# A two-layer decoder trunk on one core: DMA transposes for the second chunk of FFN parts too, and an out product ordered by chunks

## The chip, the cores and the metric

The kernel runs on one core of a Trainium2 chip. The metric is the device time of one execution in microseconds; the time before is a median of three runs. A core has TensorE (PE, matmuls and transposes), VectorE (DVE), ScalarE (ACT), GpSimd (POOL), and SyncE (SP), which here only issues DMAs.

## The reference

```python
for i in range(DEPTH):                      # 2 layers, x is 512 x 1024 float32
    h = h + 0.5 * swiglu(rms_norm(h, ffn1_norm[i]), ffn1_w_in[i], ffn1_w_out[i])
    hn = rms_norm(h, mix_norm[i])
    m = recurrent_mixer(...) if i % 2 == 0 else spatial_gating_mixer(...)
    h = h + m
    h = h + 0.5 * swiglu(rms_norm(h, ffn2_norm[i]), ffn2_w_in[i], ffn2_w_out[i])
return rms_norm(h, final_norm)

def swiglu(x, w_in, w_out):                 # w_in 1024 x 5632, w_out 2816 x 1024
    g, u = jnp.split(x @ w_in, 2, axis=-1)
    return (jax.nn.silu(g) * u) @ w_out
```

There are four FFN calls (two in each layer), and the change touches only them.

## The kernel before

**Products.** Every large matrix product is done as seven products of half-size blocks (a Strassen form, `seven`, L376): P1 P2 P5 P6 P3 P7 Q4, whose left sides are the blocks A11, A12, A22 of the left matrix and the sums S1 = A21 - A22, S2 = S1 - A11, S3 = -S2 - A22, S4 = S2 + A12 (L47, L48). The right sides are blocks of weights and their sums, made by an accumulating DMA on POOL (L139) or by an add on VectorE (L166). Each float32 operand is split into a high part (`hi`, `whi`, a copy on ScalarE) and the rest (`lo`, `wlo`, a subtract on VectorE, L103, L104, L185, L186), and each block product is three matmuls: high by high, low by high, high by low (L423 to L425). A product collects in PSUM banks A, B or C, and P6, P3 and P7 go on adding in the banks that P1 and P5 have filled (L49), once VectorE or ScalarE has read these.

**An FFN call** is cut into three parts (`FF_PARTS`, L31). Part 1 has a narrow pair and a chunk of four blocks of 128 columns; parts 2 and 3 have two chunks of four. A chunk (`chunk`, L804) runs the seven products of x with two halves of 512 rows (two entries of `cuts`), 14 steps of 12 matmuls each. Its end is the gated activation, rows of tokens, in four tiles (128 tokens by 512 columns): the first two after P3 (`p3`, L830), the other two after Q4 (`q4`, L841). After both chunks comes the part's out product (`out_blocks`, L640), again 14 steps, P1 of the first chunk, P1 of the second, P2 of the first and so on: its left side is the activation with the columns on the partitions, so the tiles have to be transposed.

**Two ways to transpose** (`left_blocks`, L752). The first chunk of parts 2 and 3, and the pair, go by the DMA (`cross`, L298): ScalarE takes the float32 tile apart into two planes of 16 bits (`planes`, L302), SyncE issues a transposing DMA for each (`move`, L310), ScalarE puts the planes together again (`merge`, L318), and VectorE makes S1 from A21 and A22 (`s1`, L322). The second chunk goes over TensorE (`stage`, L335, `turn`, L262): 16 transposes of 128x128 in two runs of eight, one step after P3 and one after Q4; ScalarE copies the result out of PSUM, and VectorE makes S1 on the way (`take`, L271). Either way `parts` (L348) then splits the block into hi and lo.

**Order.** All is issued in an order that is written by hand. The list `subs` holds the steps; the main loop (L1629) goes through them. In step i it first runs the functions hooked to "pre", then splits the weights of step i + 3, then runs "mid" and "rest", issues weight loads (L136) while fewer than eight raw buffers are in use, issues the matmuls of step i, then runs "end", the step's own work after its matmuls (`post`) and "late". Every engine works through its instructions in this order. There are four buffers of split weights, so whi of step i + 3 can be written when step i - 1 is done. `out_blocks` hooks the splits of S2, S4, S3 and A22 two steps ahead of the products that use them (three or four in some places, L732 to L736), and `sums` (L789) hooks the making of S2, S4 and S3.

**After the out product** of the last part, a norm follows (`BlockNorm.quarter`, L544): when P2 is through, ScalarE squares a quarter of x, TensorE transposes it, and so on for the other quarters.

Of the kernel before, what the change touches and what calls it, by code (L numbers as in the profile page):

```python
# [10 lines left out]
U16 = mybir.dt.uint16  # L11
# [42 lines left out]
def trunk(ctx: ExitStack, tc: tile.TileContext, a: dict, out: bass.AP):  # L54
# [13 lines left out]
    def nm(s):  # L68
        uid[0] += 1
        return f"{s}_{uid[0]}"  # L70
# [25 lines left out]
    def act(o, x, f, **k):  # L96
        nc.scalar.activation(out=o, in_=x, func=f, **k)  # L97
# [151 lines left out]
    class Group:  # L249


        def __init__(self, n):
            self.n, self.f, self.hl = n, {}, {}

        def new(self, name):
            self.f[name] = slot(name=name.lower())[:, : self.n * H]
# [38 lines left out]
            for c, g in cs:  # L295
                stt(lo[:, c], ps[:, c], g, f32(hi[:, c]), ALU.mult, ALU.subtract)

        def cross(self, n, names, tiles):  # L298

            w, pl, dt = 4 * self.n * P, [], {}  # L300

            def planes():  # L302
                for h in tiles:
                    t = sp.tile([P, 2 * T], U16, tag="s", name=nm("pl"))[:, :w]
                    act(t.rearrange("p (k b f) -> p k b f", k=2, b=2),
                        h.bitcast(U16).rearrange("p (k f b) -> p k b f", k=2, b=2), AF.Copy)
                    pl.append(t)
                tiles.clear()

            def move():  # L310
                for name, k in names:
                    d = dt[name] = sp.tile([P, 2 * T], U16, tag="s", name=nm("dt"))[:, :w]
                    v = d.rearrange("p (m s t) -> p m s t", s=2, t=P)
                    for s, t in enumerate(pl):
                        nc.sync.dma_start_transpose(out=v[:, :, s, :], in_=t[:, k * w // 2 : (k + 1) * w // 2])
# [9 lines left out]
            hook(n, "mid", planes)  # L325
            hook(n, "rest", move)
            for i, (name, _) in enumerate(names):
                hook(n + 3 + i, "mid", lambda name=name: merge(name))
                if name in ("A11", "A12"):
                    hook(n + 5 + i, "mid", lambda name=name: self.parts(name))  # L330
            if names[-1][0] == "A21":
                hook(n + 5, "pre", s1)
                hook(n + 5, "mid", lambda: self.parts("S1"))

        def stage(self, n, name, src, gains=None, parts=True, where=None, direct=0, turn=None, lag=0):  # L335

# [579 lines left out]
    def ffn(w_in, w_out, norm):  # L916
        f0 = 0
        for i, sizes in enumerate(FF_PARTS):
            groups, p0, pair, first = [], f0, None, not subs
            for j, n in enumerate(sizes):  # L920
# [10 lines left out]
            last, mixed = i == len(FF_PARTS) - 1, "p" in sizes  # L931
# [3 lines left out]
            gs = out_blocks(w_out, p0, [g.n for g in groups], 0.5, norm if last else None, own=True, soon=soon,  # L935
                            swap=mixed, p2_lag=6 * mixed)
            gs.update(enumerate(groups))


# [732 lines left out]
```

## Time and profile before

| what | value |
|---|---|
| median of three runs | 1595.22 us (1595.11 to 1600.31) |
| the profiled execution's own time | 1601.47 us |
| its span, first to last instruction | 1599.8 us |
| granted TensorE clock | 0.999 |
| DMA transposes issued by SyncE | 96 |
| share of 16 DMA engines: SyncE's queue, POOL's queue | 40.0%, 34.4% |

A group row reads: line, engine, operation, out<-in, shapes, count | busy us, mean ns of one | idle time of the engine just before, and what ended it. A row of a timeline reads: start us, length us, engine, line, operation, names, shapes, count, and in brackets the idle time before it. A row of waits reads: who waited for whom: us in total, times, the longest. Matmuls overlap, so the listed length of one is more than the time from one to the next. L97 and L88 are the helpers through which ScalarE and VectorE operations go.

### The profile page before, as it was taken

Reading aid. Unit: us, or ns where it says so; the run is one execution under the profiler, and the core shown is the slowest. Engines: PE = TensorE matmul, PEld = TensorE weight load, DVE = VectorE, ACT = ScalarE, POOL = GpSimd, SP = SyncE. Lnnn points to the kernel's source line nnn. Section 1 sums busy time; section 2 is a strip of 40 time slices with the busy share of each in tenths; the row PEclk is TensorE's granted clock in tenths of the full one; section 3 lists DMA queues with packets and bytes.
Section 4 is the critical chain, followed back from the end, with each engine's and each line's share of the span. In section 5 each row is a group of like instructions: output and inputs, shape, how many; then the busy total and the mean of one; then the engine's idle time right before and its main releaser. Section 6 shows DMA issues by size and latency. Waiting matters only on the chain.

```text
span 1599.8 us, 20767 instructions
## 1 busy us (share of the span) xinstructions
PE 1585.2 (99%) x7293; PEld 1314.5 (82%) x7293; DVE 1368.5 (86%) x1834; ACT 1098.4 (69%) x1567; POOL 223.1 (14%) x201
## 2 busy tenths in 40 slices
PE   9999999999999999999999999999999999999998
PEld 7778888898888888888788888888888888888886
DVE  6898897888998897877888978878978988889788
ACT  7757657668777657557677576576886875675676
POOL 2111111100010111111102111111211011111120
PEclk9999999999999999999999999999999999999999
DMA  8779978853294788978838788778878657796793
GB/s 287 175 170 185 226 168 193 213 150 103 82 215 104 175 189 196 220 173 174 213 112 185 177 192 213 178 179 215 226 196 207 158 127 196 179 221 173 173 223 104
DMA packets 208297, 289.79 MB, mean 181 GB/s; under 512 B 55505, under 2 KB 81217, under 8 KB 208193
## 3 DMA queue, kind: packets, MB, share of 16 engines
q1 hardware_dynamic: 158688, 195.33, 40.0%
q0 software_dynamic: 47712, 91.30, 34.4%
q10 hardware_dynamic: 1792, 1.84, 0.4%
q8 instruction: 57, 0.93, 0.2%
q14 instruction: 48, 0.39, 0.1%
HBM read 275.84 MB, written 2.10 MB: 174 GB/s over the span
## 4 chain that ended last, share of the span: by engine, by line
PE 90%; DMA 4%; DVE 3%; issue 1%; ACT 1%; SPq 0%; POOL 0%; ACTq 0%; DVEq 0%; POOLq 0%
PE A L425 13%; PE A L424 13%; PE A L423 13%; PE C L424 7%; PE C L425 7%; PE C L423 7%; PE p L870 4%; PE B L425 4%; PE B L424 4%; PE B L423 4%; PE e L268 2%; PE r L226 2%; PE r L228 2%; PE r L227 2%; DMA raw<-in_ffn_w_in_dram 2%; DMA dt<-pl 1%
## 5 line engine op out<-in xcount | busy, mean ns | idle before, releaser
L88 DVE TENSOR_TENSOR wlo<-raw,whi 128x1024 fp32r<-128x1024 f32 (+1 forms) x537 | 639.2, 1194 | 170.9 <-ACT whi L97 164.6
L97 ACT ACTIVATE whi<-raw 128x1024 fp32r<-128x1024 f32 (+1 forms) x537 | 553.7, 1034 | 324.6 <-PE A L424 81.1
L423 PE MATMUL A<-whi,hi 128*128 128x512 f32 x1016 | 399.0, 393 | 0.8 <-ACT c L97 0.8
L425 PE MATMUL A<-wlo,hi 128*128 128x512 f32 x1016 | 396.0, 390 | 0.0
L424 PE MATMUL A<-whi,lo 128*128 128x512 f32 x1016 | 395.8, 390 | 0.0
L425 PEld LDWEIGHTS A<-wlo,hi 128*128 128x128 f32 x1016 | 190.7, 188 | 40.1 <-DVE wlo L88 0.4
L423 PEld LDWEIGHTS A<-whi,hi 128*128 128x128 f32 x1016 | 190.9, 188 | 39.6 <-ACT c L97 1.2
L424 PEld LDWEIGHTS A<-whi,lo 128*128 128x128 f32 x1016 | 190.9, 188 | 38.8 <-DVE lo L88 0.3
L424 PE MATMUL C<-whi,lo 128*128 128x512 f32 x560 | 218.8, 391 | 1.2 <-DVE lo L88 1.2
L423 PE MATMUL C<-whi,hi 128*128 128x512 f32 x560 | 219.1, 391 | 0.7 <-ACT hi L97 0.7
L425 PE MATMUL C<-wlo,hi 128*128 128x512 f32 x560 | 218.7, 390 | 0.0
L139 POOL DMA_DIRECT2D raw<-in_ffn_w_in_dram x82 | 99.1, 1216 | 718.2 <-DMA raw<-in_ffn_w_out_dram 302.6
L139 POOL DMA_DIRECT2D raw<-in_ffn_w_out_dram x72 | 83.3, 1196 | 376.5 <-DVE wlo L88 152.4
L88 DVE TENSOR_TENSOR raw<-raw,raw 128x1024 f32<-128x1024 f32 x108 | 129.8, 1202 | 0.5
L88 DVE TENSOR_TENSOR lo<-a,hi 128x512 fp32r<-128x512 f32 (+1 forms) x188 | 123.0, 662 | 2.9 <-ACT hi L97 2.8
L424 PEld LDWEIGHTS C<-whi,lo 128*128 128x128 f32 x560 | 105.5, 188 | 23.9 <-DVE lo L88 2.0
L97 ACT ACTIVATE hi<-a 128x512 fp32r<-128x512 f32 (+1 forms) x188 | 111.9, 600 | 18.8 <-DVE a L88 16.6
L423 PEld LDWEIGHTS C<-whi,hi 128*128 128x128 f32 x560 | 105.4, 188 | 23.1 <-ACT hi L97 1.1
L425 PEld LDWEIGHTS C<-wlo,hi 128*128 128x128 f32 x560 | 105.6, 188 | 21.9
L424 PE MATMUL B<-whi,lo 128*128 128x512 f32 x280 | 109.1, 390 | 0.1
L423 PE MATMUL B<-whi,hi 128*128 128x512 f32 x280 | 109.1, 390 | 0.0
L425 PE MATMUL B<-wlo,hi 128*128 128x512 f32 x280 | 109.0, 389 | 0.0
(183 smaller groups left out, 2102.7 us busy)
## 6 DMA issues: line engine op xcount, KB each, us to landing
raw<-in_ffn_w_in_dram SPq DMA_DIRECT2D x161, 512.0 KB, 4.5
raw<-in_ffn_w_out_dram SPq DMA_DIRECT2D x100, 512.0 KB, 5.0
raw<-in_ffn_w_in_dram POOLq DMA_DIRECT2D x82, 512.0 KB, 6.7
raw<-in_ffn_w_out_dram POOLq DMA_DIRECT2D x60, 512.0 KB, 7.8
raw<-in_sg_w_in_dram SPq DMA_DIRECT2D x20, 512.0 KB, 6.7
raw<-in_ffn_w_in_dram SPq DMA_DIRECT2D x34, 256.0 KB, 5.1
raw<-in_rec_w_in_dram SPq DMA_DIRECT2D x16, 512.0 KB, 3.9
raw<-in_sg_w_in_dram POOLq DMA_DIRECT2D x12, 512.0 KB, 8.4
```

Of the source, the lines that this page charges most:

```text
L88: nc.vector.tensor_tensor(out=o, in0=x, in1=y, op=op)
L97: nc.scalar.activation(out=o, in_=x, func=f, **k)
L139: nc.gpsimd.dma_start(out=self.v, in_=src, accum_op=ALU.add)
L226: nc.tensor.matmul(ps, wh, xh, start=start, stop=False)
L227: nc.tensor.matmul(ps, wh, xl, start=False, stop=False)
L228: nc.tensor.matmul(ps, wl, xh, start=False, stop=stop)
L268: nc.tensor.transpose(ps[:, o : o + P], src(q, s), ident)
L423: nc.tensor.matmul(ps, zh, wh, start=fresh and i == 0, stop=False, **k)
L424: nc.tensor.matmul(ps, zl, wh, start=False, stop=False, **k)
L425: nc.tensor.matmul(ps, zh, wl, start=False, stop=end, **k)
L870: nc.tensor.matmul(bank_of(half, s), z, (sub.lo if m == 2 else sub.hi)[:, q, :], start=left[2] == "2" and (h, q, m) == (0, 0, 0), stop=lef ...
```

## The change

Three things change. (1) The second chunk of parts 2 and 3 (`late`, not in the last part of the last call) uses the DMA transposes too, with its own times: for the first half the planes come one step after P3, its merges in steps 0 and 1 of the out product, its splits in steps 1 and 2; for the second half the planes come right behind the gate, the merges at the ends of steps 3 and 5, the split of S1 in step 4. (2) The out product of these parts takes the steps in the order `APART`, so that the second chunk's P1 is step 3 (was 1), P2 step 4 (was 3), P5 step 6 (was 5), while the first chunk's P5 and P6 come at 2 and 5 (were 4 and 6). (3) In `cross` itself, for all chunks that use it: plane copies are of half a tile each, and each transpose is issued behind its own copy; S1 is made by VectorE before the planes, from the two column halves of a tile (two subtracts of 128x256); merges write in one run and read the two planes in turn (they read in one run and wrote every second 16 bits before); and for the first chunks merges, splits and sums come two steps later.

```diff
+APART = [("P1", 0), ("P2", 0), ("P5", 0), ("P1", 1), ("P2", 1), ("P6", 0), ("P5", 1), ("P6", 1), ("P3", 0), ("P3", 1),
+         ("P7", 0), ("P7", 1), ("Q4", 0), ("Q4", 1)]
...
-        def cross(self, n, names, tiles):
-            w, pl, dt = 4 * self.n * P, [], {}
-            def planes():
-                for h in tiles:
-                    t = sp.tile([P, 2 * T], U16, tag="s", name=nm("pl"))[:, :w]
-                    act(t.rearrange("p (k b f) -> p k b f", k=2, b=2),
-                        h.bitcast(U16).rearrange("p (k f b) -> p k b f", k=2, b=2), AF.Copy)
-                    pl.append(t)
+        def cross(self, half, tiles, planes, merges, parts):
+            w, names = 2 * self.n * P, ("A12", "A11") if half == 0 else ("S1", "A22")
+            if half == 0:
+                names = names[::-1]
+            dt = {}
+            def move():
+                pl = [sp.tile([P, 2 * T], U16, tag="s", name=nm("pl"))[:, : 2 * w] for _ in tiles]
+                for k, name in enumerate(names):
+                    c = slice(k * w, (k + 1) * w)
+                    d = dt[name] = sp.tile([P, 2 * T], U16, tag="s", name=nm("dt"))[:, : 2 * w]
+                    v = d.rearrange("p (m s t) -> p m s t", s=2, t=P)
+                    for s, (t, h) in enumerate(zip(pl, tiles)):
+                        act(t[:, c].rearrange("p (b f) -> p b f", b=2),
+                            h.bitcast(U16)[:, c].rearrange("p (f b) -> p b f", b=2), AF.Copy)
+                        nc.sync.dma_start_transpose(out=v[:, :, s, :], in_=t[:, c])
                 tiles.clear()
-            def move():
-                for name, k in names:
-                    d = dt[name] = sp.tile([P, 2 * T], U16, tag="s", name=nm("dt"))[:, :w]
-                    v = d.rearrange("p (m s t) -> p m s t", s=2, t=P)
-                    for s, t in enumerate(pl):
-                        nc.sync.dma_start_transpose(out=v[:, :, s, :], in_=t[:, k * w // 2 : (k + 1) * w // 2])
-                pl.clear()
             def merge(name):
-                t = self.new("S1" if name == "A21" else name)
-                act(t.bitcast(U16).rearrange("p (x b) -> p b x", b=2), dt.pop(name).rearrange("p (b x) -> p b x", b=2), AF.Copy)
-            def s1():
-                tt(self.f["S1"], self.f["S1"], self.f["A22"], ALU.subtract)
+                act(self.new(name).bitcast(U16).rearrange("p (x b) -> p x b", b=2),
+                    dt.pop(name).rearrange("p (b x) -> p x b", b=2), AF.Copy)
...
         n = now[0] + lag
+        if g.late:
+            e = now[0] + (0 if half else 4)
+            hs = [tiles[2 * half + s] for s in range(2)]
+            if half:
+                for h in hs:
+                    tt(h[:, : g.n * P], h[:, : g.n * P], h[:, g.n * P :], ALU.subtract)
+                g.cross(half, hs, (e, "late"), ((e + 4, "rest"), (e + 6, "rest")), [(e + 5, "mid")])
+                sums(g, e + 6)
+            else:
+                g.cross(half, hs, (e - 3, "mid"), ((e + 1, "mid"), (e + 2, "mid")), ((e + 2, "mid"), (e + 3, "mid")))
+            return
         if whole:
-            g.cross(n, (("A22", 1), ("A21", 0)) if half else (("A11", 0), ("A12", 1)),
-                    [tiles.pop(2 * half + s) for s in range(2)])
+            hs = [tiles[2 * half + s] for s in range(2)]
             if half:
-                sums(g, n + 6)
+                for h in hs:
+                    tt(h[:, : g.n * P], h[:, : g.n * P], h[:, g.n * P :], ALU.subtract)
+                sums(g, n + 8)
+            g.cross(half, hs, (n, "mid"), ((n + 5, "mid"), (n + 6, "mid")), [(n + 7, "mid"), (n + 8, "mid")][: 2 - half])
             return
...
+                    groups[-1].late = j == 1 and not mixed and not (last and hasattr(norm, "last"))
...
+            gs = out_blocks(w_out, p0, [g.n for g in groups], 0.5, norm if last else None,
+                            APART if groups[1].late else None, own=True, soon=soon, swap=mixed, p2_lag=6 * mixed)
```

More of the change, by code (lines that the diff above doesn't have):

```diff
@@ L252, in __init__ @@
         def __init__(self, n):
-            self.n, self.f, self.hl = n, {}, {}
+            self.n, self.f, self.hl, self.late = n, {}, {}, False
         def new(self, name):
@@ L296, in direct @@
                 stt(lo[:, c], ps[:, c], g, f32(hi[:, c]), ALU.mult, ALU.subtract)
-        def cross(self, n, names, tiles):
-            w, pl, dt = 4 * self.n * P, [], {}
-            def planes():
-                for h in tiles:
-                    t = sp.tile([P, 2 * T], U16, tag="s", name=nm("pl"))[:, :w]
-                    act(t.rearrange("p (k b f) -> p k b f", k=2, b=2),
-                        h.bitcast(U16).rearrange("p (k f b) -> p k b f", k=2, b=2), AF.Copy)
-                    pl.append(t)
-                tiles.clear()
-            def move():
-                for name, k in names:
-                    d = dt[name] = sp.tile([P, 2 * T], U16, tag="s", name=nm("dt"))[:, :w]
-                    v = d.rearrange("p (m s t) -> p m s t", s=2, t=P)
-                    for s, t in enumerate(pl):
-                        nc.sync.dma_start_transpose(out=v[:, :, s, :], in_=t[:, k * w // 2 : (k + 1) * w // 2])
-                pl.clear()
-            def merge(name):
-                t = self.new("S1" if name == "A21" else name)
-                act(t.bitcast(U16).rearrange("p (x b) -> p b x", b=2), dt.pop(name).rearrange("p (b x) -> p b x", b=2), AF.Copy)
-            def s1():
-                tt(self.f["S1"], self.f["S1"], self.f["A22"], ALU.subtract)
[L325 to L333, printed above, removed]
@@ new lines, in cross @@
+        def cross(self, half, tiles, planes, merges, parts):
[13 more added lines that the diff above has]
+                        nc.sync.dma_start_transpose(out=v[:, :, s, :], in_=t[:, c])
+                tiles.clear()
+            def merge(name):
+                act(self.new(name).bitcast(U16).rearrange("p (x b) -> p x b", b=2),
+                    dt.pop(name).rearrange("p (b x) -> p x b", b=2), AF.Copy)
+            hook(*planes, move)
+            for name, at in zip(names, merges):
+                hook(*at, lambda name=name: merge(name))
+            for name, at in zip(names, parts):
+                hook(*at, lambda name=name: self.parts(name))
@@ L919, in ffn @@
             groups, p0, pair, first = [], f0, None, not subs
+            last, mixed = i == len(FF_PARTS) - 1, "p" in sizes
             for j, n in enumerate(sizes):
@@ L934, in ffn @@
             soon = {("Q4", 1): 3} if last and isinstance(norm, TileNorm) else {}
-            gs = out_blocks(w_out, p0, [g.n for g in groups], 0.5, norm if last else None, own=True, soon=soon,
-                            swap=mixed, p2_lag=6 * mixed)
+            gs = out_blocks(w_out, p0, [g.n for g in groups], 0.5, norm if last else None,
+                            APART if groups[1].late else None, own=True, soon=soon, swap=mixed, p2_lag=6 * mixed)
             gs.update(enumerate(groups))
```

1 line of the change is left out of this document (removed).

## The prediction

> **What bounds the kernel now.** I read the page's engine busy times first, then its chain.
>
> ```profile
> span 1599.8 us, 20767 instructions
> PE 1585.2 (99%) x7293; PEld 1314.5 (82%) x7293; DVE 1368.5 (86%) x1834; ACT 1098.4 (69%) x1567; POOL 223.1 (14%) x201
> PE 90%; DMA 4%; DVE 3%; issue 1%; ACT 1%; SPq 0%; POOL 0%; ACTq 0%; DVEq 0%; POOLq 0%
> ```
>
> TensorE is busy 99% of the span and carries 90% of the chain: what leaves its queue is gained, and what makes it wait is lost. VectorE is close behind. Next, the waits of TensorE, all the transposes of FFN blocks, and a stretch of the chain in order of time:
>
> ```profile
> PE e L268 <- DVE c L94: 4.0, 8, 1.1
> ```
>
> ```profile
> L268 PE MATMUL e<-ident,c 128*128 128x128 f32 x224 | 30.7, 274 | 4.0 <-DVE c L94 4.0
> ```
>
> ```profile
> 656.52 0.87 PE e L268 x8
> ```
>
> Eight of these transposes take 0.87 us on the chain, 0.109 each (the 274 ns of the group are overlapped lengths). The only sizeable waits of TensorE stand before them. Then the busy time of each engine in one out product, that of part 2 of the second FFN call (its second chunk ends at 653.64):
>
> ```profile
> 653.64:689.89 36.25, 36.25 (x165) 30.11 (x164) 34.54 (x45) 19.69 (x25) 4.82 (x4) 1.00 0.81 204
> ```
>
> The columns are PE, PEld, DVE, ACT, POOL busy, then clock, DMA share, GB/s. TensorE has no gap, but VectorE is busy 34.54 of 36.25 us: this is the stage where the change puts its work, and VectorE has hardly anything left there.
>
> **What is removed.** Seven second chunks become "late" (parts 2 and 3 of the four FFN calls, less the very last). Each loses 16 transposes on TensorE: 7 x 2 x 0.87 = **12.2 us**. Of the waits, those of late chunks are
>
> ```profile
> 292.84 0.55 PE L268 MATMUL e<-ident,c 128*128 128x128 f32 x3 [0.50 <-DVE c L94]
> ```
>
> ```profile
> 644.64 0.98 PE L268 MATMUL e<-ident,c 128*128 128x128 f32 x7 [0.55 <-DVE c L94]
> ```
>
> ```profile
> 761.07 0.30 PE L268 MATMUL e<-ident,c 128*128 128x128 f32 x1 [0.25 <-DVE c L94]
> 762.37 0.99 PE L268 MATMUL e<-ident,c 128*128 128x128 f32 x7 [1.00 <-DVE c L94]
> ```
>
> 0.50 + 0.55 + 0.25 + 1.00 = **2.3 us**. If nothing else were late, the gain would be 14.5 us.
>
> **What is added, and its prices.**
>
> ```profile
> L97 ACT ACTIVATE whi<-raw 128x1024 fp32r<-128x1024 f32 x507 | 535.0, 1058 | 318.9 <-PE A L424 79.0 <-DVE raw L88 72.1 <-PE C L424 68.6
> L88 DVE TENSOR_TENSOR wlo<-raw,whi 128x1024 fp32r<-128x1024 f32 x507 | 618.5, 1223 | 164.7 <-ACT whi L97 158.4 <-PE e L268 4.1 <-PE A L425 1.4
> L97 ACT ACTIVATE hi<-a 128x512 fp32r<-128x512 f32 x168 | 103.8, 623 | 18.8 <-DVE a L88 16.6 <-DVE a L94 1.0
> L88 DVE TENSOR_TENSOR lo<-a,hi 128x512 fp32r<-128x512 f32 x168 | 114.6, 690 | 2.9 <-ACT hi L97 2.8
> L88 DVE TENSOR_TENSOR raw<-raw,raw 128x1024 f32<-128x1024 f32 x104 | 127.0, 1221 | 0.5
> L94 DVE SCALAR_TENSOR_TENSOR x<-A,x 128x512 f32<-128x512 f32 x112 | 71.8, 689 | 6.4 <-PE A L425 6.3
> L88 DVE TENSOR_TENSOR a<-y,h 128x256 f32<-128x256 f32 x16 | 5.8, 422 | 0.0
> L97 ACT ACTIVATE pl<-h 128x512 uint16<-128x512 uint16 x16 | 9.0, 612 | 0.0
> L97 ACT ACTIVATE pl<-c 128x1024 uint16<-128x1024 uint16 x32 | 32.9, 1054 | 2.7 <-DVE c L94 2.6
> L97 ACT ACTIVATE a<-dt 128x1024 uint16<-128x1024 uint16 x24 | 32.9, 1372 | 19.0 <-DMA dt<-pl 18.8
> L97 ACT ACTIVATE junk<-x 128x512 f32<-128x512 f32 x55 | 34.1, 625 | 7.8 <-DVE x L94 7.5
> L97 ACT ACTIVATION_READ_ACCUMULATOR junk<-x 128x1 f32 x55 | 10.5, 191 | 0.0
> ```
>
> Per late chunk ScalarE gets 8 plane copies of 128x512 (0.61 us) and 4 merges, and loses three copies from PSUM; VectorE gets two 128x256 subtracts (0.42) for one 128x512 operation. The merge in its new order (one run written, two planes read in turn) isn't in the trace. Its bounds are 1.05 (plane copy: strided read, one written run) and 1.37 (old merge: strided write); I take 1.05, since what the change turns round is the write, as in the plane copy. The Trainium skill ("Advanced Engine Details and Errata", SBUF Cachelines) says that an access which leaves the 16-byte line each time pays a penalty; the new merge's read does. No row here shows that case; it is a rival below.
>
> The first chunks change too: two plane copies become four of half size (2.1 to 2.4 us), merges and parts two products later. Their merges now wait 19.0 us for the DMA on ScalarE; that wait goes, but TensorE never waited there but for the transposes counted above, so I cost it at nothing. The cover is the weight splits made three products ahead, 8 us; were that gone, TensorE would see at most those 19 us, and they get fewer, not more.
>
> SyncE's queue: 56 more DMA transposes stand ahead of later loads.
>
> ```profile
> SPq L136 <- DVE wlo L88: 932.5, 266, 16.8
> ```
>
> ```profile
> dt<-pl SPq DMA_TRANSPOSE x96, 3.8
> ```
>
> ```profile
> L315 SPq DMA_TRANSPOSE dt<-pl x96: 1182/1252/3072, 45.4 to 1523.3; - x96
> ```
>
> SyncE spends 932 us waiting for free buffers, and in the program's order each load behind the new transposes is first used seven or more products (19 us) later; a transpose lands in 3.8. The new order of products also reorders the loads of the out product (P5's first block comes third), but each still goes out six or more products ahead of its split, and its accumulating load on POOL, two products behind the load, still has six products (16 us) to land. I cost the queues at nothing; without that lead it would be four issues of 1.25 us for each half, 5 us.
>
> **The stage that pays.** Let E be the end of the late chunk's last product, and number the out product's steps 0 to 13; a step takes 2.72 us. The rows of that stage today:
>
> ```profile
> 653.84 0.69 ACT L97 ACTIVATE s<-A,rt 128x512 f32<-128x512 f32 x1 [0.67 <-PE A L425]
> 654.42 1.05 ACT L97 ACTIVATE whi<-raw 128x1024 fp32r<-128x1024 f32 x1
> 666.18 1.06 ACT L97 ACTIVATE whi<-raw 128x1024 fp32r<-128x1024 f32 x1 [2.41 <-DVE raw L88]
> ```
>
> ```profile
> 654.07 1.41 DVE L94 SCALAR_TENSOR_TENSOR c<-c,rt,s 128x512 f32<-128x512 f32 x2
> 655.51 1.23 DVE L88 TENSOR_TENSOR wlo<-raw,whi 128x1024 fp32r<-128x1024 f32 x1
> 670.05 0.69 DVE L88 TENSOR_TENSOR lo<-a,hi 128x512 fp32r<-128x512 f32 x1
> ```
>
> ```profile
> 653.64 0.39 PE L423 MATMUL A<-whi,hi 128*128 128x512 f32 x1
> ...
> 670.85 0.39 PE L423 MATMUL A<-whi,hi 128*128 128x512 f32 x1
> ...
> 673.57 0.39 PE L423 MATMUL A<-whi,hi 128*128 128x512 f32 x1
> ```
>
> E is 653.64, where step 0 starts. The last two rows give the step (2.72, twelve matmuls of 0.23). Step 6 starts at 670.85, and its second matmul needs the lo that ends at 670.74: 0.34 us to spare, today. Operations on one engine start some 0.09 before the listed end of the one ahead (the two gates of 0.75 take 1.41), which the sums below use. The order of instructions on each engine is that of the changed program.
>
> *Product 3 (P1, second chunk).* The last tile's gate (c<-c,rt,s) ends at E+1.7 to 1.8. Now two subtracts follow (E+2.3), and only then can the four planes run, in ScalarE's queue ahead of the next weight split: they end at E+4.2, and whi of product 3 starts at E+4.1 where it stood at E+0.8. Behind it: merge A11 to 6.1, whi(4) to 7.1, merge A12 to 8.0, hi of A11 to 8.6, its lo on VectorE to 9.3. Before the change A11 and A12 are split before E, from PSUM. Product 3 is due at 8.16, its second matmul at 8.39: **0.95 late**.
>
> *Product 6 (P5, second chunk).* VectorE runs without a break from here: wlo(5) to 10.8, lo A12 11.4, wlo(6) 12.5, lo S2 13.1, P1's two updates of x 13.7 and 14.3 (step 5, P6, adds into those banks from 14.6 on: just in time), the add of two weight blocks 15.4. whi(7) waits for that add (as at 666.18), to 16.5, wlo(7) 17.8, and lo of S1 stands behind it: 18.4. The second matmul is due at 0.95 + 16.32 + 0.23 = 17.5: **0.94 late**.
>
> *Products 7 and 8.* P2's updates 19.6, s2 20.2, hi S2 20.9, wlo(8) 21.3, lo S2 21.9, against 21.2: **0.8**. s4 22.5, wlo(9) 24.0, lo S4 24.6, P5's first update of x 25.2; product 8 adds into that bank, due at 24.5: **0.8**. Product 10 loses another **0.2**. Sum 3.7 us (4.6 with a merge of 1.37).
>
> Before a norm (three of seven), two squares (0.63 and 0.19 for the accumulator) and two more lo's land at products 5 to 8, one step later than today: product 8 then loses 1.35 and product 10 0.8, in all 4.9 (5.8).
>
> So 4 x 3.7 + 3 x 4.9 = **29.5 us** lost; less 14.5, **+15.0**. The profiled execution took 1601.47 (its span 1599.8); the same shift on the median 1595.22 gives **1610**.
>
> **Rivals.** *The covers hold* (faster): the transposes go and TensorE waits nowhere. It decides if product 3's lo A11 is there by E+8.4, that is, if ScalarE is 0.95 us earlier than I count, and product 6's by the same measure. For it: 31% of ScalarE is idle on average. Against it: its order is fixed, and it idles waiting for the gate just there. 1595.2 - 14.5 = 1581.
>
> *The stalls about pay for the transposes:* only products 3 and 6 are late (1.9 per part, 13 us), updates of x slip in without harm: 1594; with 1 to 2.9 per part, 1588 to 1601.
>
> *The merge is dear:* at an estimated twice the plane copy (2.1) the same count gives 6.9 and 8.1 per part, 52 us, net +37: 1632. That is what the skill's rule on lines would do; nothing in the trace decides it.
>
> *Transposes land late.* The Trainium skill ("VectorE: DVE Perf Modes", The three transpose paths) prefers TensorE for 128x128 where PSUM will do. Here S1's merge comes at E+11.5, the second transpose's issue at E+4.4: it costs nothing below 7 us of flight, and each us above it only eats ScalarE's 3 us before whi(7). I count it into the upper end.
>
> **Numbers.** Forecast (net +8 to +23: 1603 to 1618) 0.60; covers hold 0.13; stalls pay 0.17; dear merge or late landing 0.10. The range leaves out half of the "covers hold" and of the dearest cases: **1587 to 1622**. A measurement can tell about 0.5% (8 us): faster 0.14, same 0.18, slower 0.68.
>
> **What would show it.** Group e<-ident,c at x112. TensorE waiting before A in product 3 (for lo or hi), before C in product 6 and again in 7 and 8, for VectorE, seven times each, 25 to 36 us in all. ScalarE's whi after the gate starting some 4 us behind E. Merge rows near 1.05. If TensorE shows no waits in out products, the count of ScalarE's queue is wrong; if VectorE is idle there, its load was not the cause.

## The result and the profile after

The changed kernel takes **1620.92 us** (median of 4 runs, 1620.81 to 1622.8) beside 1596.41 for the kernel before on the same chip (4 runs, 1595.11 to 1600.31): ratio 1.0146, 95% interval 1.0131 to 1.0162. It is slower by 24.5 us. The forecast was 1610 in a range of 1587 to 1622.

The page of the changed kernel first. Line numbers have moved: ScalarE's and VectorE's helpers are L99, L90 and L96, the transposes of TensorE L270, the three matmuls L417 to L419.

```profile
span 1619.2 us, 20901 instructions
PE 1584.7 (98%) x7181; PEld 1298.9 (80%) x7181; DVE 1370.6 (85%) x1853; ACT 1142.1 (71%) x1678; POOL 222.2 (14%) x201
PE 86%; DVE 6%; ACT 4%; DMA 2%; issue 2%; SPq 0%; ACTq 0%; DVEq 0%
```

TensorE has 112 instructions fewer and yet the same busy time, and its share of the chain fell from 90% to 86%, while VectorE's and ScalarE's rose to 6% and 4%. (A matmul in front of which TensorE waited is listed with 0.50 where others have 0.39, so busy time hides part of a wait.) Next, what TensorE waited for, over the whole span:

```profile
PE C L417 <- DVE x L96: 9.1, 7, 2.5
PE C L418 <- DVE lo L90: 6.2, 8, 1.2
PE A L418 <- DVE lo L90: 5.0, 14, 0.6
PE A L417 <- ACT hi L99: 3.8, 7, 0.5
```

The counts are the argument: seven late parts, and 7, 8, 14 and 7 waits. The waits for a gated tile before transposes (`e` for `c`), 4.0 us in 8 before the change, have no row any more. The groups that the change touches:

```profile
L270 PE MATMUL e<-ident,c 128*128 128x128 f32 x112 | 14.6, 272 | 0.0
L99 ACT ACTIVATE a<-dt 128x1024 uint16<-128x1024 uint16 x45 | 52.7, 1170 | 0.0
```

Half of the 224 transposes are gone. A merge in its new order takes 1.17 us, and none waits for the DMA (the last column, the idle time of ScalarE ahead of them, is 0.0).

Now the stage that the prediction took apart, the out product of part 2 of the second FFN call. Its late chunk ends at 656.90, which is E. First the busy times of the engines from E to the start of step 13 (653.64 to 689.89 before):

```profile
656.90:696.54 39.64, 36.95 (x158) 28.88 (x156) 34.21 (x46) 25.95 (x34) 4.82 (x4) 1.00 0.91 211
```

It was 36.25 with eight transposes (0.87) in it; it is 39.64 without any. ScalarE's busy time rose from 19.69 to 25.95. The rows of TensorE in that stage, cut to the first matmul of some steps and to those with a wait:

```profile
656.90 0.39 PE L417 MATMUL A<-whi,hi 128*128 128x512 f32 x1
...
665.76 0.50 PE L417 MATMUL A<-whi,hi 128*128 128x512 f32 x1 [0.54 <-ACT hi L99]
...
666.49 0.50 PE L418 MATMUL A<-whi,lo 128*128 128x512 f32 x1 [0.22 <-DVE lo L90]
...
669.11 0.39 PE L417 MATMUL B<-whi,hi 128*128 128x512 f32 x1
...
674.55 0.39 PE L417 MATMUL C<-whi,hi 128*128 128x512 f32 x1
...
675.65 0.50 PE L418 MATMUL C<-whi,lo 128*128 128x512 f32 x1 [0.71 <-DVE lo L90]
...
678.28 0.40 PE L417 MATMUL A<-whi,hi 128*128 128x512 f32 x1
...
679.18 0.50 PE L418 MATMUL A<-whi,lo 128*128 128x512 f32 x1 [0.51 <-DVE lo L90]
...
682.68 0.47 PE L417 MATMUL C<-whi,hi 128*128 128x512 f32 x1 [0.71 <-DVE x L96]
...
696.54 0.39 PE L417 MATMUL Q<-whi,hi 128*128 128x512 f32 x1
```

A step without a wait takes 2.72, so step 13 is due at 656.90 + 13 x 2.72 = 692.26; it starts at 696.54, **4.28 late**. By the same arithmetic step 4 (669.11, due 667.78) starts 1.33 late, and step 6 (674.55, due 673.22) no later; step 7 starts 1.01 later still, and step 8 another 1.68, of which 0.81 falls into step 7 and 0.87 ahead of step 8. The waits in brackets add up to 2.69 only. The rest hides in the listed lengths (0.39 for a matmul whose successor could start after 0.23) and in the restarts: the matmul behind a waiting one starts up to 0.34 after it, not 0.23, which is some 0.11 us each time.

What ScalarE does in the first nine microseconds, from the planes on:

```profile
658.94 2.19 ACT L99 ACTIVATE pl<-c 128x512 uint16<-128x512 uint16 x4 [1.15 <-DVE c L90]
661.04 1.04 ACT L99 ACTIVATE whi<-raw 128x1024 fp32r<-128x1024 f32 x1
661.99 1.17 ACT L99 ACTIVATE a<-dt 128x1024 uint16<-128x1024 uint16 x1
663.06 1.05 ACT L99 ACTIVATE whi<-raw 128x1024 fp32r<-128x1024 f32 x1
664.01 1.17 ACT L99 ACTIVATE a<-dt 128x1024 uint16<-128x1024 uint16 x1
665.09 0.61 ACT L99 ACTIVATE hi<-a 128x512 fp32r<-128x512 f32 x1
```

Before the planes it idles 1.15 us for the subtracts, and then four planes, two weight splits and two merges stand in a row in front of hi of A11, which TensorE wants at 665.06 (step 3, E + 8.16).

VectorE, the three rows that TensorE waits for in steps 6, 7 and 8:

```profile
674.91 0.68 DVE L90 TENSOR_TENSOR lo<-s,hi 128x512 fp32r<-128x512 f32 x1
...
678.45 0.68 DVE L90 TENSOR_TENSOR lo<-a,hi 128x512 fp32r<-128x512 f32 x1
...
681.85 1.28 DVE L96 SCALAR_TENSOR_TENSOR x<-C,x 128x512 f32<-128x512 f32 x2
```

### The profile page after: what moved, and what is told of

Read it like the earlier page. It is cut to its first block, busy times and chain, and to the rows that moved or that the text cites. A ratio compares the mean times of both kernels' runs of the same rounds, so it can differ in the third digit from the quotient of the medians.

```text
span 1619.2 us, 20901 instructions
## 1 busy us (share of the span) xinstructions
PE 1584.7 (98%) x7181; PEld 1298.9 (80%) x7181; DVE 1370.6 (85%) x1853; ACT 1142.1 (71%) x1678; POOL 222.2 (14%) x201
## 4 chain that ended last, share of the span: by engine, by line
PE 86%; DVE 6%; ACT 4%; DMA 2%; issue 2%; SPq 0%; ACTq 0%; DVEq 0%
PE A L417 13%; PE A L418 13%; PE A L419 13%; PE C L417 7%; PE C L418 7%; PE C L419 7%; PE p L877 5%; PE B L418 3%; PE B L419 3%; PE B L417 3%; ACT whi L99 2%; PE r L228 2%; PE r L230 2%; PE r L229 2%; PE e L270 2%
## 5 line engine op out<-in xcount | busy, mean ns | idle before, releaser
L90 DVE TENSOR_TENSOR wlo<-raw,whi 128x1024 fp32r<-128x1024 f32 (+1 forms) x537 | 637.4, 1189 | 193.2 <-ACT whi L99 191.0
L99 ACT ACTIVATE whi<-raw 128x1024 fp32r<-128x1024 f32 (+1 forms) x537 | 553.6, 1032 | 289.7 <-DVE raw L90 76.1
L417 PE MATMUL A<-whi,hi 128*128 128x512 f32 x1016 | 400.2, 394 | 4.4 <-ACT hi L99 3.8
L419 PE MATMUL A<-wlo,hi 128*128 128x512 f32 x1016 | 396.0, 390 | 0.0
L417 PEld LDWEIGHTS A<-whi,hi 128*128 128x128 f32 x1016 | 190.7, 188 | 51.6 <-ACT hi L99 6.9
L417 PE MATMUL C<-whi,hi 128*128 128x512 f32 x560 | 219.1, 391 | 10.5 <-DVE x L96 9.1
L419 PEld LDWEIGHTS A<-wlo,hi 128*128 128x128 f32 x1016 | 190.7, 188 | 39.9 <-DVE wlo L90 0.5
L419 PE MATMUL C<-wlo,hi 128*128 128x512 f32 x560 | 218.2, 390 | 0.0
L99 ACT ACTIVATE hi<-a 128x512 fp32r<-128x512 f32 (+1 forms) x188 | 111.7, 598 | 34.5 <-DVE a L90 32.8
L417 PEld LDWEIGHTS C<-whi,hi 128*128 128x128 f32 x560 | 105.1, 188 | 35.7 <-ACT hi L99 13.8
L90 DVE TENSOR_TENSOR raw<-raw,raw 128x1024 f32<-128x1024 f32 x108 | 129.4, 1198 | 1.0
L90 DVE TENSOR_TENSOR lo<-a,hi 128x512 fp32r<-128x512 f32 (+1 forms) x188 | 122.0, 655 | 3.0 <-ACT hi L99 2.1
L419 PEld LDWEIGHTS C<-wlo,hi 128*128 128x128 f32 x560 | 105.1, 188 | 21.6
L417 PE MATMUL B<-whi,hi 128*128 128x512 f32 x280 | 109.0, 389 | 0.0
L419 PE MATMUL B<-wlo,hi 128*128 128x512 f32 x280 | 108.9, 389 | 0.0
```

Source lines behind the costliest of these rows:

```text
L90: nc.vector.tensor_tensor(out=o, in0=x, in1=y, op=op)
L417: nc.tensor.matmul(ps, zh, wh, start=fresh and i == 0, stop=False, **k)
L419: nc.tensor.matmul(ps, zh, wl, start=False, stop=end, **k)
```

## The experiments

The theory was the prediction's, with the sizes that the profile gave: the work that stands behind the gate makes TensorE wait in step 3 for ScalarE, and in steps 6 to 8 for VectorE's queue. Rivals were that the order APART, the changed form of the first chunks, or the load on the DMA costs the time. Ratios are to the kernel before on the same chip; spans are of one profiled execution each. Another execution of the kernel before was profiled as the base, since the first one was 3.5 us behind it by its first 100 us:

> The kernel before once more, for a second trace of it: the seven out products and the waits before transposes as in the first trace; the first 100 us, where its first trace shows 10 us of TensorE waiting, may differ by some us.

Its span is 1596.8, and its transposes waited as follows:

```profile
PE e L268 <- DVE c L94: 4.6, 6, 1.1
```

### One part alone: the form of the first chunks

```diff
-                    groups[-1].late = j == 1 and not mixed and not (last and hasattr(norm, "last"))
+                    groups[-1].late = False
```

> The changed transposing code for the first chunks alone (half planes, S1 made before the planes, merges in the new order and two products later); second chunks go over TensorE and the out product has its old order. Theory (the whole loss comes from the late chunks' work behind the gate): TensorE loses nothing here and is rid of some of the 2.3 to 3 us that it waited for VectorE before the transposes: about 3 us faster than before, -4 to 0. Rival (the changed code of the first chunks costs a share of the loss): 5 us or more slower than before.

Measured: 1595.55, ratio 0.9973 (0.9961 to 0.9984), span 1594.1. All 224 transposes are there (the order is the old one too), yet no wait before them is left in the profile:

```profile
L270 PE MATMUL e<-ident,c 128*128 128x128 f32 x224 | 29.3, 272 | 0.0
```

So those waits, of which the prediction took off 2.3 us for the late chunks, go with the first chunks' new form and not with the transposes. Which of its parts does it (half planes, the early S1, the merge order, the later merges) this run doesn't tell. By itself it is a gain of 3 to 6 us by the interval, and the kernel with it alone is the fastest of all that were run.

### One part alone: the order

The kernel before with APART in the seven out products, transposes on TensorE as they were.

```diff
+APART = [("P1", 0), ("P2", 0), ("P5", 0), ("P1", 1), ("P2", 1), ("P6", 0), ("P5", 1), ("P6", 1), ("P3", 0), ("P3", 1),
+         ("P7", 0), ("P7", 1), ("Q4", 0), ("Q4", 1)]
...
+                            None if mixed or (last and hasattr(norm, "last")) else APART, own=True, soon=soon,
```

> The new order of products alone, in the same seven out products; all else as before. Theory: A11 and A12 are split before the out product starts, so steps 3 and 4 wait for nothing, and the same count of VectorE's queue gives at most 0.7 us late in a part that is not before a norm: 0 to 4 us slower than before. Rival (the order itself makes products late, whatever transposes): 15 us or more slower than before.

Measured: ratio 1.0046 (1.0028 to 1.0063), span 1601.2: 4 to 10 us by the interval, more than the 0 to 4 expected, but short of the rival's 15. TensorE's two largest waits:

```profile
PE e L270 <- DVE c L96: 3.3, 5, 1.0
PE A L426 <- DVE lo L90: 3.3, 5, 0.8
```

The second row is new and lies in step 7, before a lo of VectorE: even without the crossbar the order brings lo of the second chunk's S2 close to its use. The prediction had no separate price for the order.

### The change without the order

```diff
-                            APART if groups[1].late else None, own=True, soon=soon, swap=mixed, p2_lag=6 * mixed)
+                            None, own=True, soon=soon, swap=mixed, p2_lag=6 * mixed)
```

> As the changed kernel, with the out product in its old order (second chunk's P1 at step 1). Theory (A11 of the second chunk is there at 9.3 us behind the gate's product whatever the order): step 1, due at 2.7, waits some 6.5 us, by the count 7.7 us in each of seven parts, 54 us, less the 15 for transposes and waits: 36 to 42 us slower than before. Rival (the new order is what costs): faster than the changed kernel, 5 to 15 us slower than before.

Measured: 1660.63, ratio 1.0374 (1.0347 to 1.0401), 62 us and not 36 to 42. The direction was right, and the excess has a cause of its own. The first of seven waits, and the granted clock (the number after POOL's busy time) before, behind and further behind it:

```profile
190.52 0.79 PE L417 MATMUL A<-whi,hi 128*128 128x512 f32 x1 [5.95 <-ACT hi L99]
```

```profile
180.00:185.00 5.00, 4.57 (x21) 3.44 (x19) 3.52 (x8) 2.70 (x6) 0.00 (x0) 1.00 1.20 118
...
190.00:195.00 5.00, 4.48 (x10) 3.27 (x11) 1.59 (x4) 0.46 (x1) 1.97 (x2) 0.50 1.17 282
```

Seven waits of 5.95 are 41.6 us, and behind each the clock is halved for 4 to 6 us. So the order is not the culprit: it takes most of the wait for A11 away, and the change without it would be far worse.

### Planes of the second half behind the next weight split

```diff
-                g.cross(half, hs, (e, "late"), ((e + 4, "rest"), (e + 6, "rest")), [(e + 5, "mid")])
+                g.cross(half, hs, (e + 1, "mid"), ((e + 4, "rest"), (e + 6, "rest")), [(e + 5, "mid")])
```

> As the changed kernel, but the second half's planes stand behind the next weight split in ScalarE's queue, not ahead of it. Theory (whi of product 3 stands behind planes that wait for the gate, and all that follows is late by it): each of the seven out products loses 1.2 us less, by the count 2.9 and 4.1 for 4.1 and 5.3: 8 to 9 us faster than the changed kernel, some 14 to 16 us slower than before; step 3 waits less, steps 6 to 8 still do. Rival (the transposes land late, or the load on the DMA engines does it): no change from the changed kernel, 24 us slower than before.

Measured: 1612.6, ratio 1.0077 (1.0058 to 1.0097), span 1610.3, 8.9 less than the changed kernel. TensorE's three largest waits:

```profile
PE C L417 <- DVE x L96: 9.1, 7, 2.5
PE C L418 <- DVE lo L90: 6.3, 8, 1.2
PE A L418 <- DVE lo L90: 2.5, 5, 0.6
```

The row before A for hi is gone, that for lo fell from 14 waits to 5, and the first two stand as they were. Step 3 is ScalarE's queue, and steps 6 to 8 are something else.

### Is it the DMA?

Each transpose of a late half is issued once more, into a buffer that nothing reads, in one run right behind its original (the first lines), in another behind all four (the last lines).

```diff
+                        if self.late:
+                            x = sp.tile([P, 2 * T], U16, tag="s", name=nm("again"))[:, :w].rearrange("p (m t) -> p m t", t=P)
+                            nc.sync.dma_start_transpose(out=x, in_=t[:, c])
...
+                for t in pl if self.late else ():
+                    for k in range(2):
+                        x = sp.tile([P, 2 * T], U16, tag="s", name=nm("again"))[:, :w].rearrange("p (m t) -> p m t", t=P)
+                        nc.sync.dma_start_transpose(out=x, in_=t[:, k * w : (k + 1) * w])
```

> As the changed kernel, with every transpose of the late chunks issued a second time into a scratch tile (56 more). Theory (ScalarE's and VectorE's queues decide, the DMA has slack): within 3 us of the changed kernel, 24 us slower than before. Rival (the DMA engines or SyncE's queue decide): the transposes' share of the loss comes a second time, 10 us or more on top of the changed kernel.

Measured: 1638.33, ratio 1.0224 (1.0198 to 1.0251), some 17 us over the changed kernel: a miss for the theory as it stood. ScalarE's waits for a landing and TensorE's largest:

```profile
ACT a L99 <- DMA dt<-pl: 11.1, 7, 2.9
```

```profile
PE C L420 <- DVE x L96: 20.9, 7, 4.1
```

With the copies in between, A22's transposes go out later, its merge waits up to 2.9 us, and step 8 waits longer (behind each of these waits the granted clock was halved too, see the last section). The changed kernel has no such wait, so this shows only how little the transposes of the second half may slip. Whether it was the order in the queue or the load was told apart by the second form:

> The changed kernel with four more DMA transposes for each half of a late chunk, issued behind the four real ones and not in between, of which nothing is read. It separates what the doubled transposes of the run before measured: the order in SyncE's queue (A22's transposes went out behind the copies of S1's) or the load on the DMA engines. Theory (it was the order; the DMA's load costs nothing that TensorE sees): within 3 us of the changed kernel, 22 to 28 us over the kernel before, with no wait for the DMA ahead of ScalarE's merges of a half that stands out. Rival (every transpose beside the out product's loads makes what else is in flight late, so that the change pays for its DMA traffic): 10 us or more over the changed kernel again, as in the run before.

Measured: 1621.46, ratio 1.0142 (1.0122 to 1.0161), the changed kernel's time, with TensorE's largest wait as it was:

```profile
PE C L421 <- DVE x L96: 9.1, 7, 2.5
```

The same 56 transposes more, and nothing lost: the DMA's load is not what the change pays for.

### Is it VectorE's queue?

The four updates of x behind the second chunk's P1 and P2 are left out in late parts; their sums are missing in x, so the output is not the reference's.

```diff
+        skip = order is APART
...
-            upd(s, 0, ps, scale)
+            if not skip:
+                upd(s, 0, ps, scale)
```

> The changed kernel without the four updates of x (0.69 us each on VectorE) behind the second chunk's P1 and P2 in the seven late out products: these two products' sums are left out of x there, so the output is not the reference's. Theory (TensorE waits in steps 6 to 8 because VectorE's queue, full since the subtracts and splits moved behind the gate, runs the lo's late): the waits of step 3 stay, those of steps 6 to 8 shrink to a third or less; by the same count as the prediction's a plain part loses 1.7 us in place of 4.1 and a part before a norm 2.9 in place of 5.3, 17 us less than the changed kernel, about 6 us over the kernel before. Rival (steps 6 to 8 wait for ScalarE's merges, for the DMA or for accumulating weight loads): within 5 us of the changed kernel, 18 or more over the kernel before.

Measured: 1604.44, ratio 1.0040 (1.0028 to 1.0051), span 1602.3: 16.9 us less than the changed kernel, as counted. TensorE's waits:

```profile
PE A L417 <- ACT hi L99: 3.8, 7, 0.5
PE C L417 <- DVE x L96: 3.5, 5, 2.0
PE A L418 <- DVE lo L90: 2.4, 9, 0.4
...
PE C L418 <- DVE lo L90: 1.2, 1, 1.2
```

Step 3's wait stays at 3.8 in seven; the waits before C fell from 9.1 and 6.2 to 3.5 and 1.2. (One wait of 1.2 before C for lo stands in the kernel before too, early in the run.) So most of the waiting in steps 6 to 8 is for a VectorE that is full, and 4 x 0.6 us of work per part is what it takes.

### Only the first half over the crossbar

A11 and A12 by DMA transposes, A22 and A21 back on TensorE, once in the old order with merges in the last step of the chunk and step 0, once with APART and the merges one product later.

```diff
-                for h in hs:
-                    tt(h[:, : g.n * P], h[:, : g.n * P], h[:, g.n * P :], ALU.subtract)
-                g.cross(half, hs, (e, "late"), ((e + 4, "rest"), (e + 6, "rest")), [(e + 5, "mid")])
-                sums(g, e + 6)
+                g.stage(n, "A22", src(1, 2), None, False)
+                g.stage(n + 1, "A21", src(0, 2), turn=n)
+                sums(g, n + 3)
...
-                g.cross(half, hs, (e - 3, "mid"), ((e + 1, "mid"), (e + 2, "mid")), ((e + 2, "mid"), (e + 3, "mid")))
+                g.cross(half, hs, (e - 3, "mid"), ((e, "mid"), (e + 1, "mid")), ((e, "rest"), (e + 1, "rest")))
...
-                            APART if groups[1].late else None, own=True, soon=soon, swap=mixed, p2_lag=6 * mixed)
+                            None, own=True, soon=soon, swap=mixed, p2_lag=6 * mixed)
```

The first lines are common to both; those behind the first dots are of the run in the old order alone.

> Only the first half of the late chunks (A11 and A12, two tiles that are ready four products before the out product) goes by DMA transposes; the second half stays on TensorE, the order of the out product is the old one, and the first chunks have their new form. This saves 56 transposes of 0.109 us (6.1 us) and puts no operation behind the gate of the last tiles. Theory (what is dear is the work behind the gate and the full queue of VectorE after it, not the DMA way as such): the gain of the first chunks alone (about 3 us) and 3 to 6 us more, ratio 0.993 to 0.996 to the kernel before, with no wait of TensorE in steps 0 to 3. Rival (ScalarE's four planes of 0.61 and two merges of 1.17 make whi late wherever they stand, or the transposes do): equal to the kernel before or slower, ratio 1.000 or more.

Measured: 1639.76, ratio 1.0253 (1.0231 to 1.0274), a clear miss. ScalarE's row of A11's merge in one stage, and TensorE's one large wait:

```profile
665.96 1.17 ACT L99 ACTIVATE a<-dt 128x1024 uint16<-128x1024 uint16 x1 [6.27 <-DMA dt<-pl]
```

```profile
PE e L270 <- DVE c L96: 30.2, 8, 5.5
```

The merge sits in ScalarE's queue ahead of the scaling for the last gate and waits 6.27 us for its two transposes. These were issued at 651.87 and 653.59 and landed at 665.24 and 665.88, 13.4 and 12.3 us later, while two accumulating loads of POOL were in flight (issued at 649.62 and 652.06, landed at 659.50 and 665.39). ScalarE was ready at 659.69, 7.8 us behind the first issue. So the experiment doesn't test the theory; it tests a lead of some 8 us, and finds that it isn't enough there. (In the changed kernel A11's merge starts 14.6 us behind the first issue. In the first mended version below, which has APART, it starts 7.7 us behind, at 648.73, and waits for nothing: so it is what the old order has in flight there, not the lead alone.) With the order APART and the merges a product later:

> The changed kernel with the second half of the late chunks (A22 and A21, whose tiles end last) back on TensorE; the first half goes by DMA transposes with its merges in steps 0 and 1, one product later than in the run with the old order, which waited 6 us for a landing each time. So 56 transposes (6.1 us) are gone, nothing stands behind the gate, and no merge waits for the DMA. Theory (the dear part of the change is what stands behind the gate): the order alone cost 4 to 7 us, the first chunks' form gave 3 back, the transposes give 6, so -6 to +1 us, ratio 0.996 to 1.001, no wait in step 3 and steps 6 to 8 no later than with the order alone. Rival (the merges and planes on ScalarE, or the landing of the transposes, cost wherever they stand): 8 us or more over the kernel before, ratio 1.005 or more, with waits for hi or for the transposes in steps 3 to 5.

Measured: 1599.17, ratio 1.0004 (0.9994 to 1.0013, twelve runs), span 1597.7. TensorE's largest wait is that of the order:

```profile
PE A L418 <- DVE lo L90: 4.4, 6, 1.0
```

This is the experiment that places the loss. From here to the changed kernel only the second half moves, from TensorE to the DMA, and the span goes from 1597.7 to 1619.2: **21.5 us**, though 56 more transposes (6.1 us) go. The ratios, 1.0004 and 1.0146, say 23 us. Its waits are therefore worth some 27.6 us. The run itself doesn't come out at the sum of its parts, though: 1596.8 less 2.7 (first chunks) plus 4.4 (order) less 6.1 would be 1592.4. The 5 us more may be what the first half's crossbar costs, but single executions of the kernel before differ by as much, and it was not traced further.

### Two mended versions

First the planes later, the merges and splits of A11 and A12 earlier (the merges by one product), and S2 and S4 moved; then, on top, the second chunk's P5 ahead of the first chunk's P6, whose weight blocks are then added by an accumulating DMA, not by VectorE (S1 and A12 are split a little earlier there too). The lines are those of the first.

```diff
-                g.cross(half, hs, (e, "late"), ((e + 4, "rest"), (e + 6, "rest")), [(e + 5, "mid")])
-                sums(g, e + 6)
+                g.cross(half, hs, (e + 1, "mid"), ((e + 4, "rest"), (e + 6, "rest")), [(e + 5, "mid")])
+                hook(e + 5, "rest", g.s2)
+                hook(e + 7, "pre", g.s4)
+                hook(e + 8, "pre", g.s3)
...
-                g.cross(half, hs, (e - 3, "mid"), ((e + 1, "mid"), (e + 2, "mid")), ((e + 2, "mid"), (e + 3, "mid")))
+                g.cross(half, hs, (e - 3, "mid"), ((e, "mid"), (e + 1, "mid")), ((e, "rest"), (e + 2, "mid")))
```

> As the changed kernel, with four functions moved in the order: the second half's planes behind the next weight split, A11's merge and split ahead of the gate, A12's merge a step earlier, and S2 made ahead of P2's updates of x. Theory (each lateness comes from what stands ahead in ScalarE's and VectorE's queues): 1.4 us left in a plain part and 1.9 before a norm, 11 us, less 15: 2 to 6 us faster than before. Rival (the work itself is too much for ScalarE and VectorE there, or the DMA decides): 10 us or more slower than before.

Measured: 1600.3, ratio 1.0004 (0.9991 to 1.0017): 20 us better than the changed kernel, but no better than the kernel before, against an expected 2 to 6 us. Now ScalarE does wait for landings, and TensorE still waits in step 8, 6.0 us where the changed kernel has 9.1:

```profile
ACT s L99 <- DMA dt<-pl: 7.6, 5, 2.1
ACT a L99 <- DMA dt<-pl: 2.8, 1, 2.8
```

```profile
PE C L417 <- DVE x L96: 6.0, 7, 2.4
```

In the stage that was looked at, A22's merge waits 2.76 us for its landing, and step 8, behind it by way of VectorE's queue, waits 2.39. What the other six waits come from was not traced.

> As the mended kernel, with P5 of the second chunk ahead of P6 of the first, so that P6 of the first chunk gets its weight block by an accumulating DMA and VectorE is spared one add of 1.2 us in each of the seven out products; one accumulating DMA of 512 KB more each; S1 and A12 split a little earlier. Theory (VectorE's queue is what is left): nearly no waiting, 0 to 0.3 us a part: 12 to 15 us faster than before. Rival (the DMA engines, 0.81 to 0.96 busy there, are late with the added block): step 6 waits for VectorE behind the DMA, and the time is that of before or worse.

Measured: 1640.85, ratio 1.025 (1.0221 to 1.028), where 12 to 15 us of gain were expected. The rival was right: VectorE's add is gone, and the accumulating load that replaces it is late. ScalarE's wait, and TensorE's behind it:

```profile
ACT whi L99 <- DMA raw<-in_ffn_w_out_dram: 41.6, 8, 7.4
```

```profile
PE C L417 <- ACT hi L99: 28.9, 8, 6.5
```

## Why the prediction held, and where it was short

The mechanism and its places were as forecast. The loss was 24.5 us and not 15, so the time lies only 1 us inside the upper end of the range, and the range's width had its share in that. Times of the stage above, from E = 656.90:

| what | predicted | in the trace |
|---|---|---|
| last gate ends | 1.7 to 1.8 | 1.67 |
| subtracts end | 2.3 | 2.34 |
| planes end; whi of product 3 starts | 4.2; 4.1 | 4.23; 4.14 |
| merges A11 and A12 end | 6.1; 8.0 | 6.26; 8.28 |
| lo of A11 ends | 9.3 | 9.53 |
| lo of S1 ends | 18.4 | 18.69 |
| lo of S2 ends | 21.9 | 22.23 |
| steps 3, 6, 7, 8, 10 lose | 0.95, 0.94, 0.8, 0.8, 0.2 | 1.33, 1.01, 0.81, 0.99, 0.14 |
| a plain part; one before a norm | 3.7; 4.9 | 4.3 to 4.6; 5.5 to 6.0 |

**Removed: 12.2 us of transposes.** Right (112 left). **2.3 us of waits before them.** The waits went, 4.6 us of them in the second profile of before, but the first chunks' form alone takes them away; the prediction had put that form at nothing.

**The dear stage: 29.5 us.** It measured about 34.8 us, summed over the seven out products from the starts of TensorE's instructions; the waits that the profile lists in the four rows above add up to 24.1 (1.2 of it from elsewhere), just short of the 25 to 36 that the prediction named as its sign. The mechanism was right, and this term was too small by some 5 us for three reasons. The merge takes 1.17 and not 1.05, so lo of A11 ends 0.23 later. The prediction counted lateness only up to the arrival of lo, which in the trace is 9.53 less 8.39, 1.14 us; the waiting matmul starts 0.06 after that, and those behind it lose another 0.13 until they are back at their pace. And before a norm it put 1.35 and 0.8 on steps 8 and 10 together with the earlier waits: the trace has 2.0 to 2.7 at step 8 (the longest wait before C is 2.54).

**The sum.** 34.8 less 12.2 less 4.6 makes 18.0; some 2 us of small waits outside the seven products come on top. The two spans differ by 22.4 (1619.2 and 1596.8). About 2 us stay unplaced, and the medians differ by 2 more than these two executions do.

**Covers at nothing.** That SyncE's queue and the loads pay nothing held: the merges wait 0.0, and 56 transposes more cost nothing when issued last. The reason given, a landing in 3.8 us, did not hold: beside the out product's loads the second halves' transposes took 3.5 to 8.1 us in the changed kernel, most of them over 5, and up to 14.0 in the run with the first half only. The second transpose of S1 was issued at 660.88 and landed at 667.68, and the merge that reads it starts at 668.55:

```profile
668.55 1.16 ACT L99 ACTIVATE s<-dt 128x1024 uint16<-128x1024 uint16 x1
```

It had 0.87 us to spare. The rival on late landings had put that bound at 7 us of flight (the merge 7.1 behind the issue); the trace shows 6.8 of flight and 7.7 between issue and merge. It cost nothing, by little.

**The dear merge** is out: 1.17 is 11% over a plane copy of that size and not twice. The 2.1 us of that rival was an estimate that no row bore out. The Trainium skill ("Advanced Engine Details and Errata", SBUF Cachelines) says that an access that leaves its line each time pays a penalty; in these traces the merge that reads two planes in turn takes 0.12 us more than the plane copy's 1.05, and the old merge with its strided write took 0.32 more.

**The other side** (covers hold) asked for ScalarE to be 0.95 us earlier; the run with the planes behind the next weight split gives just that in step 3, and steps 6 to 8 remained.

## What to carry to other kernels

To take work off the engine that bounds a kernel is worth it only where the replacement's own chain has room at that point: the half of this change on tiles that are ready four products early cost about nothing on balance, and the same edit on the tiles that end last cost 21.5 us. Count the fixed queues of the other engines operation by operation from the event that releases them to the instruction that needs them; in the plain part that count came within 0.4 us at every point. A work-free time in the average (31% of ScalarE before the change) says nothing of the queue right behind a gate.

## What the runs showed of the hardware

A long wait of TensorE is paid twice. Behind the waits of 5.95 us the granted clock read 0.50 (above), for 4 to 6 us each; the matmuls start 0.43 us apart there in place of 0.23. That is an estimated 2.5 us for each wait, some 17 us in all, most of what the run without the order lost beyond its count. A much shorter wait can do the same. This is the longest wait of the changed kernel, and the same wait in the run with the extra transposes behind, each with the clock after it:

```profile
328.26 0.47 PE L417 MATMUL C<-whi,hi 128*128 128x512 f32 x1 [2.54 <-DVE x L96]
```

```profile
327.49:330.90 3.41, 2.63 (x12) 2.18 (x13) 3.41 (x6) 1.63 (x4) 0.00 (x0) 1.00 0.51 149
```

```profile
328.55 0.57 PE L421 MATMUL C<-whi,hi 128*128 128x512 f32 x1 [2.55 <-DVE x L96]
```

```profile
328.77:332.18 3.41, 3.41 (x9) 2.62 (x9) 3.41 (x6) 2.52 (x4) 0.00 (x0) 0.50 1.15 347
```

The Trainium skill ("TensorE: Matmul & The Clock Gate", HAM oscillation — how this bites in real kernels) puts the bound at gaps of about 3.4 us. Here less was enough: 2.55 and 2.63 us in the two runs with extra transposes, 1.97 in the run without updates, and 1.86 in the run with the planes later (ended at 797.12):

```profile
798.40:801.81 3.41, 3.41 (x10) 2.63 (x9) 3.41 (x6) 2.91 (x5) 0.00 (x0) 0.50 0.46 123
```

So no length of a single wait is the bound; where it falls seems to decide. In the traces' clock records every stretch at half speed before the end of the run lasts 3.41 or 6.83 us, and within a run these stretches start a multiple of 3.41 apart (208.36, 331.24 and 689.64 with the doubled transposes: 36 and 105 times). The four waits named lie within one stretch of such a grid, right before the slow one (that of 2.63 but for its first 0.31). In the changed kernel the grid, counted back from its only slow record (1617.73, at the end), has a border at 327.49, and cuts the wait of 2.54 us into 1.77 and 0.77. How much idle time within one stretch is needed isn't settled: a wait of 1.86 us within one (ending at 1137.70 in the run with the extra transposes behind) left the clock at 1.00. So a change that lengthens a wait to 2 us or more can lose more than the wait.

And a DMA transpose of 128 KB, whose median from issue to landing is 4.3 us in the changed kernel, took 12.3 and 13.4 in the run with the first half only, beside two accumulating loads. In the changed kernel accumulating loads were in flight too, beside transposes of 6 to 8 us, so which transfers make one late was not separated. A lead of 7.7 us was enough in the first mended version, and one of 7.8 was not in the run with the first half only.
